# PEER expert layer: the second products of the last four expert blocks by token tile, and one copy of the final norm's weights for two gathered tiles

## The chip, the core and the metric

The program runs on one core of one Trainium2 chip. The metric is the device time of one execution in microseconds. Before the change it was measured three times: 3582.51, 3587.91 and 3587.44 us, median 3587.44.

## What is computed

One decoder layer on 1024 tokens of width 1024 and a last RMSNorm: a token mixer with three branches (stick-breaking attention, sparse attention, a gated recurrence), then a layer of 16384 experts (PEER) of which each token uses 128. The change lies in the PEER layer and in the last norm. Cut to that:

```python
def peer_ffn(x, w_q, sub_keys, u_tab, v_tab):
    ...
        eidx = jnp.take_along_axis(cand_idx, pos, axis=-1)
        gate = jax.nn.softmax(best_s, axis=-1)
        ug = u_tab[eidx]
        vg = v_tab[eidx]
        hpre = jnp.einsum("nd,nhkd->nhk", xc, ug).astype(f32)
        act = (gate * jax.nn.gelu(hpre, approximate=False)).astype(x.dtype)
        return jnp.einsum("nhk,nhkd->nd", act, vg)
...
        x = x + peer_ffn(h, peer_w_q[l], peer_sub_keys[l], peer_u[l], peer_v[l])
    return rms_norm(x, norm_final)
```

## The kernel before

The tokens lie in four parts of 256, that is eight tiles of 128. The mixer handles the parts one after the other. The PEER layer is computed in two ways at the same time.

**Tiles 2 to 5 (512 tokens) are dense.** All 16384 experts are computed for them, in 128 blocks of 128 experts (the loop of L1409). The first product of a block (`gemm1`, L1380) loads 512 KB of the table u, splits it into two f16 halves (`split`, L210: the high half on ACT, L213, the rest on DVE, L214), runs 24 matmuls of 128x512 (L258) and a Gelu on ACT (L1390). It runs three blocks ahead of the rest (LEAD). Then the block's rows of v are loaded (`vraw`, two buffers) and split the same way (`vs`, a tile with the tag "v", six buffers); DVE multiplies the Gelu's result by the gates (L1424, "the gating" below), which are mostly zero and come from DRAM in `gt` tiles for eight blocks (three buffers); the result is split into `ac` (five buffers). The second product (`gemm2`, L1427) adds the block to the output: for a token tile t of the four and a half dh of the width, three matmuls. Six of the eight outputs of 128x512 have a PSUM bank of their own (`accs`) that collects over all 128 blocks, 18 matmuls a block. The fourth tile (t = 3) has none: every four blocks, 24 matmuls go into a bank of the first products' pool (`ps_mm`), ACT copies it out (L1440) and DVE adds it to `acc7` (L1441). After the loop, for t = 0 to 3, DVE adds the scaled output to the residual `yd` (L1460), `rms_scale` (L218 to L233) forms the norm's factor with a square on ACT (L223) and steps of 128x1 on DVE and ACT, DVE multiplies by the factor and the weights `gfd` (L1462), and SP stores (L1463).

**Tiles 0, 1, 6 and 7 gather** (`gather_tile`, L1133). For each of its 128 columns an indirect DMA, issued by POOL, fetches for every token the row of u that it uses (L1145, 512 KB), and DVE multiplies it with the token's vector and sums it up (L1147). ACT applies the Gelu (L1149), DVE the gates (L1151). Then 128 rows of v come in the same way (L1155), and DVE adds each into `gacc` (L1157). The norm follows (L1160), with its weights loaded into `gf` (L1161), the multiply (L1162) and the store (L1163). Tiles 6 and 7 run beside the second half of the dense loop, one after the other. Their rows rotate through eleven buffers (`late_rows`, L1075): four of five with the tag "rows", four halves of two larger tiles (named `rr_u`, `rr_v`), and three freed tiles. The tag "rows" also holds `gh2`, `gacc`, the square's junk and `gf`.

**What sets the order.** Each engine executes one list in order. The lists are laid out when the kernel is built: the framework's scheduler simulates the program with its own costs, picks what is ready, and inserts the waits. A buffer that comes free later moves everything that wants it, and all that the scheduler places after it. Lines under `paced()` (the gathers' DVE operations) are further held to a pace.

Of the kernel before, what the change touches and what calls it, by code (L numbers as in the profile page):

```python
# [10 lines left out]
F32 = mybir.dt.float32  # L11
# [5 lines left out]
AF = mybir.ActivationFunctionType  # L17
ALU = mybir.AluOpType
# [16 lines left out]
D = 1024  # L35
TH = 512
# [28 lines left out]
PARTS = [Part(i, i * 256, 256) for i in range(4)]  # L65
# [6 lines left out]
def trunk(ctx: ExitStack, tc: tile.TileContext, a: dict, out: bass.AP):  # L72
    nc = tc.nc
    V, S, G, P = nc.vector, nc.scalar, nc.gpsimd, nc.tensor
# [10 lines left out]
    ps_mm = ctx.enter_context(tc.tile_pool(name="ps_mm", bufs=2, space=PSUM))  # L85
# [9 lines left out]
    def log_exp():  # L95

        tc.keep_in_program_order(S.preload_act_table_set(LOG_EXP))

    def load(t, src):
        nc.sync.dma_start(t, src)  # L100
        return t

    def W4(name, shape=(128, 1024), dt=F32):
        return w4.tile(list(shape), dt, tag="w4", name=name)

    def W2(name, shape=(128, 512), dt=F32, tag="at", bufs=AT):
        return (wk if tag in ("at", "pre", "sg") else w2).tile(list(shape), dt, tag=tag, name=name, bufs=bufs)
# [103 lines left out]
    def split(hi, lo, src, scale):  # L211

        S.activation(hi, src, AF.Copy, scale=scale)  # L213
        V.scalar_tensor_tensor(lo, in0=src, scalar=scale, in1=hi, op0=ALU.mult, op1=ALU.subtract)  # L214
# [855 lines left out]
    def rows(name):  # L1070
        return gat.tile([128, D], F32, tag="rows", name=name, bufs=RB)
# [43 lines left out]
    def paced():  # L1115

        if not paces:
            def rows(tau):
                return [tau * (p + PB) if k >= PACE0 else 0.0 for k, (_, v, p) in enumerate(marks)]

            lo, hi = 0.0, 10.0
            for _ in range(40):
                mid = (lo + hi) / 2
                lo, hi = (mid, hi) if sum(rows(mid)) < PACE else (lo, mid)
            acc = 0.0
            for m, r in zip(marks, rows(lo)):
                acc += r
                paces.extend([m[0]] * (int(acc) - len(paces)))
            paces.append(marks[-1][0])
            paces.append(0)  # L1130
        k = paces[-1]
        paces[-1] += 1
        return tc.issue_after(paces[min(k, len(paces) - 2)])  # L1133

    def gather_tile(ti):
        row = late_rows if ti // 2 == PARTS[-1].i else rows
        h2 = load(rows(f"gh2_{ti}"), d_h2[ti])
        idx = load(gat.tile([128, 128], I32, tag="gidx", name=f"gidx_{ti}", bufs=1), d_idx[ti])
        gate = load(gat.tile([128, 128], F32, tag="ggate", name=f"ggate_{ti}", bufs=2), d_gate[ti])
        hpre = gat.tile([128, 128], F32, tag="hpre", name=f"hpre_{ti}", bufs=1)  # L1140
        G.memset(hpre, 0.0)
        act = gat.tile([128, 128], F32, tag="act", name=f"act_{ti}", bufs=1)
        for c in range(128):
            ur = row(f"u{ti}_{c}")
            G.indirect_dma_start(out=ur, out_offset=None, in_=a["peer_u"], in_offset=bass.IndirectOffsetOnAxis(ap=idx[:, c:c + 1], axis=0))  # L1145
            with paced():
                V.scalar_tensor_tensor(ur, in0=ur, scalar=1.0, in1=h2, op0=ALU.mult, op1=ALU.mult, accum_out=hpre[:, c:c + 1])  # L1147
        with tc.high_priority():
            S.activation(act, hpre, AF.Gelu)  # L1149
            log_exp()  # L1150
        V.tensor_tensor(act, act, gate, op=ALU.mult)  # L1151
        acc = load(rows(f"gacc_{ti}"), d_x2[ti])
        for c in range(128):
            vr = row(f"v{ti}_{c}")
            G.indirect_dma_start(out=vr, out_offset=None, in_=a["peer_v"], in_offset=bass.IndirectOffsetOnAxis(ap=idx[:, c:c + 1], axis=0))  # L1155
            with paced():
                V.scalar_tensor_tensor(acc, in0=vr, scalar=act[:, c:c + 1], in1=acc, op0=ALU.mult, op1=ALU.add)  # L1157
        with tc.high_priority():
            log_exp()
        y = rms_scale(acc, f"fin{ti}", rows(f"sqf{ti}"), "g")  # L1160
        gf = load(rows(f"gf{ti}"), a["norm_final"].to_broadcast([128, D]))  # L1161
        V.scalar_tensor_tensor(acc, in0=acc, scalar=y, in1=gf, op0=ALU.mult, op1=ALU.mult)  # L1162
        nc.sync.dma_start(out[ti * 128:(ti + 1) * 128, :], acc)  # L1163

# [35 lines left out]
    NI = 128  # L1200
# [64 lines left out]
    for pt in PARTS:  # L1265
        i = pt.i
# [73 lines left out]
    t = 0  # L1340
# [41 lines left out]
    def gemm1(i):  # L1382

        ge = W2(f"ge{i}")
        ps = ps_mm.tile([128, TH], F32, tag="mm", name=f"g1_{i}")
        raw = load(W4(f"uraw{i}", (128, 8, 128)), a["peer_uT"][i])
        u = wpl.tile([128, 2, 8, 128], F16, tag="wp", name=f"us{i}", bufs=WB)
        split(u[:, 0], u[:, 1], raw, SW)
        mm3(ps, (u[:, 0], u[:, 1]), (h2[:, 0], h2[:, 1]), 8)
        S.activation(ge, ps, AF.Gelu, scale=1.0 / (SW * SH2))  # L1390
        return ge
# [8 lines left out]
    accs = [ps_a.tile([128, 512], F32, name=f"acc{i}") for i in range(6)]  # L1400
    acc7 = late.tile([128, 2, 512], F32, name="acc7")
    V.memset(acc7, 0.0)
    group = []
# [2 lines left out]
    gts = {}  # L1406
    ys = []
    gone = 0
    for k, i in enumerate(order):  # L1409
        if k + LEAD < NI:  # L1410
            ges[order[k + LEAD]] = gemm1(order[k + LEAD])
        raw = load(late.tile([128, D], F32, tag="vraw", name=f"vraw{i}", bufs=2), a["peer_v"][i * 128:(i + 1) * 128, :])
        v = late.tile([128, 2, D], F16, tag="v", name=f"vs{i}", bufs=6)
        split(v[:, 0], v[:, 1], raw, SW)
        if i // 8 not in gts:
            gts[i // 8] = []
            for c in (0, 16):
                gt = late.tile([128, 16, 8, 16], F32, tag="gt", name=f"gt{i}_{c}", bufs=3)
                nc.sync.dma_start(gt, d_G[c:c + 16, :, i // 8 * 8:i // 8 * 8 + 8, :].rearrange("c p i n -> p c i n"))
                gts[i // 8].append(gt)  # L1420
        ge = ges.pop(i)
        for c, gt in enumerate(gts[i // 8]):
            gv = ge[:, c * 256:c * 256 + 256].rearrange("p (c n) -> p c n", n=16)
            V.tensor_tensor(gv, gv, gt[:, :, i % 8, :], op=ALU.mult)  # L1424
        ac = late.tile([128, 2, TH], F16, tag="ac", name=f"ac{i}", bufs=5)
        split(ac[:, 0], ac[:, 1], ge, 1.0)
        group.append((ac, v))  # L1427

        def gemm2(ps, t, dh, ac, v, start, stop):
            for n, (x, y) in enumerate(((0, 0), (0, 1), (1, 0))):  # L1430
                P.matmul(ps, ac[:, x, t * 128:(t + 1) * 128], v[:, y, dh * 512:(dh + 1) * 512], start=start and n == 0, stop=stop and n == 2)  # L1431

        for u in range(6):
            if u in (2, 4) and len(group) == 4:
                d0 = u // 2 - 1
                ps = ps_mm.tile([128, TH], F32, tag="mm", name=f"g2_{i}_{u}")
                for n, (x, y) in enumerate(group):
                    gemm2(ps, 3, d0, x, y, n == 0, n == 3)
                part = W2(f"p7_{i}_{u}")
                S.activation(part, ps, AF.Copy)  # L1440
                V.tensor_tensor(acc7[:, d0], acc7[:, d0], part, op=ALU.add)  # L1441
                if d0:
                    group = []
            gemm2(accs[u], u // 2, u % 2, ac, v, k == 0, k == NI - 1)

        if k + LEAD >= NI:
            ys.append(load(W4(f"yd{len(ys)}"), d_x2[DENSE[0].ti0 + len(ys)]))
            if k == NI - 1:
                ys.append(load(W4("yd3"), d_x2[DENSE[0].ti0 + 3]))
                gfd = load(late.tile([128, D], F32, tag="v", name="gfd", bufs=6), a["norm_final"].to_broadcast([128, D]))  # L1450

        while ending and gone < (k + 1) * TP:
            ending.pop(0).emit(1 << 20)
            gone += 1
    log_exp()
    for t in range(4):
        y = ys[t]
        for dh in range(2):
            yv = y[:, dh * 512:(dh + 1) * 512]
            V.scalar_tensor_tensor(yv, in0=(accs[t * 2 + dh] if t < 3 else acc7[:, dh]), scalar=1.0 / (SW * SA), in1=yv, op0=ALU.mult, op1=ALU.add)  # L1460
        r = rms_scale(y, f"find{t}", late.tile([128, D], F32, tag="vraw", name=f"sqd{t}", bufs=2))
        V.scalar_tensor_tensor(y, in0=y, scalar=r, in1=gfd, op0=ALU.mult, op1=ALU.mult)  # L1462
        nc.sync.dma_start(out[TD + t * 128:TD + (t + 1) * 128, :], y)  # L1463
# [96 lines left out]
```

## Time and profile before

| | us |
|---|---|
| median of three runs | 3587.44 |
| lowest and highest | 3582.51, 3587.91 |
| the profiled execution | 3598.97 |
| its span in the profile | 3597.2 |
| PE busy | 3273.4 (91%) |
| DVE busy | 3002.8 (83%) |
| ACT busy | 1588.9 (44%) |
| POOL busy | 1342.3 (37%) |

The profile is of one execution, 11.53 us longer than the median of the others; 1.8 us of it lie outside the span. PE is the matmul engine, DVE the vector engine, ACT the one for activations, POOL issues the gathers and SP the other loads and stores. A busy share over the whole span says little here: the stages have different limits, and the stretch that the change touches is the last 300 us or so, in which PE, DVE and the DMA engines are all nearly full.

### The profile page before, as it was taken

To read this page: it belongs to the slowest core of one execution; us is meant where nothing else is said; L and a number is where in the kernel's file an instruction comes from. 1 tells how busy PE (TensorE), PEld (TensorE's weight loads), DVE (VectorE), ACT (ScalarE), POOL (GpSimd) and SP (SyncE) were. 2 spreads that over 40 slices of the span, in tenths; PEclk is the share of its full clock that TensorE was granted. 3 is DMA by queue.
4 is the path that set the end of the run, shared out by engine and by line. 5 is a ranking of instruction groups with operands and counts; after the bars stand their busy time and mean duration, and the time that the engine had idled before them with its cause. 6 is when DMAs were issued, how large, how long until landed. Compare 5 with 4: busy or idle time off the path is not lost.

```text
span 3597.2 us, 57076 instructions
## 1 busy us (share of the span) xinstructions
PE 3273.4 (91%) x20660; PEld 2191.4 (61%) x20660; DVE 3002.8 (83%) x6662; ACT 1588.9 (44%) x3157; POOL 1342.3 (37%) x1166
## 2 busy tenths in 40 slices
PE   7999989989997889999878879879999999999997
PEld 6887777778875667787666645434444444444443
DVE  5565678888799878788997777999897998898898
ACT  5776455653443554645356333224233333333333
POOL 0000002343323323223332233346674765666664
PEclk9999999999996889999677789989999999999998
DMA  8964856989977577887665799789998999999997
GB/s 300 329 237 143 303 185 224 329 300 328 351 259 230 198 248 244 306 320 261 218 201 184 265 348 316 240 270 374 358 369 316 383 378 343 379 358 364 352 343 263
DMA packets 358760, 1053.88 MB, mean 293 GB/s; under 512 B 35174, under 2 KB 107562, under 8 KB 354380
## 3 DMA queue, kind: packets, MB, share of 16 engines
q0 software_dynamic: 147456, 536.94, 41.7%
q1 hardware_dynamic: 211020, 513.29, 40.2%
q8 instruction: 162, 2.65, 0.3%
q14 instruction: 122, 1.00, 0.1%
HBM read 942.09 MB, written 108.00 MB: 292 GB/s over the span
## 4 chain that ended last, share of the span: by engine, by line
PE 44%; DVE 24%; DMA 11%; issue 10%; ACT 7%; POOL 4%; SPq 0%; POOLq 0%; DVEq 0%; ACTq 0%
PE g L258 11%; PE acc L1431 8%; DVE u L1147 4%; PE pj_mg L258 3%; DVE gacc L1157 3%; PE g L1431 3%; DMA d_G<-stage 3%; PE pj_r_hg L258 3%; DMA v<-in_peer_v_dram,gidx 2%; PE pb L258 2%; DMA u<-in_peer_u_dram,gidx 2%; PE pj_wo L258 2%; POOL v L1155 2%; DMA gt<-d_G 1%; POOL u L1145 1%
## 5 line engine op out<-in xcount | busy, mean ns | idle before, releaser
L1155 POOL DMA_INDIRECT v<-in_peer_v_dram,gidx x421 | 541.5, 1286 | 723.1 <-DVE gacc L1157 435.6
L1145 POOL DMA_INDIRECT u<-in_peer_u_dram,gidx x417 | 523.7, 1256 | 683.2 <-DVE u L1147 440.2
L258 PE MATMUL g<-h,us 128*128 128x512 f16 x3072 | 692.0, 382 | 26.3 <-DVE ts L982 10.3
L1157 DVE SCALAR_TENSOR_TENSOR gacc<-v,act,gacc 128x1024 f32<-128x1024 f32 x421 | 538.5, 1279 | 35.1 <-DMA v<-in_peer_v_dram,gidx 31.6
L1431 PE MATMUL acc<-vs,ac 128*128 128x512 f16 x2304 | 540.3, 383 | 23.1 <-DVE vs L214 9.7
L1431 PEld LDWEIGHTS <-ac 128*128 128x128 f16 x3072 | 303.2, 99 | 419.2 <-issue 58.7
L258 PEld LDWEIGHTS <-us 128*128 128x128 f16 x3072 | 302.1, 98 | 395.3 <-issue 24.8
L1147 DVE SCALAR_TENSOR_TENSOR u<-u,gh 128x1024 f32<-128x1024 f32 x417 | 501.6, 1218 | 33.1 <-DMA u<-in_peer_u_dram,gidx 30.0
L1390 ACT ACTIVATE ge<-g 128x512 f32<-128x512 f32 x128 | 76.2, 595 | 570.6 <-PE g L258 528.2
L258 PE MATMUL pj_mg<-hT,w_mg 128*128 128x256 f16 x2304 | 276.3, 276 | 8.8 <-ACT mg L883 7.0
L258 PEld LDWEIGHTS <-w_mg 128*128 128x128 f16 x2304 | 228.7, 100 | 40.1 <-issue 12.6
L1431 PE MATMUL g<-vs,ac 128*128 128x512 f16 x768 | 187.4, 386 | 24.6 <-ACT ge L1390 23.0
L1221 ACT ACTIVATE stage<-gb 128x512 f32<-128x512 f32 x128 | 130.3, 1070 | 125.3 <-DMA d_G<-stage 59.9
L214 DVE SCALAR_TENSOR_TENSOR vs<-vraw,vs 128x1024 f16<-128x1024 f32 x128 | 155.5, 1218 | 35.5 <-ACT vs L213 35.3
L213 ACT ACTIVATE vs<-vraw 128x1024 f16<-128x1024 f32 x128 | 133.0, 1046 | 82.4 <-DMA vraw<-in_peer_v_dram 79.6
L258 PE MATMUL pb<-o,w_b 128*128 128x256 f16 x1152 | 147.8, 286 | 21.4 <-DVE sg L921 12.7
L1145 POOL DMA_INDIRECT rr_u<-in_peer_u_dram,gidx x95 | 132.6, 1396 | 85.6 <-DVE rr_u L1147 62.7
L1155 POOL DMA_INDIRECT rr_v<-in_peer_v_dram,gidx x90 | 128.6, 1428 | 95.5 <-DVE gacc L1157 72.4
L214 DVE SCALAR_TENSOR_TENSOR us<-uraw,us 128x1024 f16<-128x1024 f32 x128 | 155.9, 1218 | 9.8 <-ACT us L213 9.4
L1218 PE MATMUL gb<-hot 128*128 128x128 f16 x512 | 125.3, 294 | 42.1 <-ACT stage L1221 22.3
L213 ACT ACTIVATE ac<-ge 128x512 f16<-128x512 f32 x128 | 79.7, 627 | 176.0 <-DVE ge L1424 122.3
L1424 DVE TENSOR_TENSOR ge<-ge,gt 128x256 f32<-128x256 f32 x256 | 98.6, 422 | 68.0 <-ACT ge L1390 46.2
(1143 smaller groups left out, 6439.4 us busy)
## 6 DMA issues: line engine op xcount, KB each, us to landing
uraw<-in_peer_uT_dram SPq DMA_DIRECT2D x128, 512.0 KB
vraw<-in_peer_v_dram SPq DMA_DIRECT2D x128, 512.0 KB
w_mg<-dw SPq DMA_DIRECT2D x72, 512.0 KB
d_G<-stage SPq DMA_DIRECT2D x32, 1024.0 KB
gt<-d_G SPq DMA_DIRECT2D x32, 1024.0 KB
w_r_hg<-dw SPq DMA_DIRECT2D x36, 512.0 KB
w_b<-dw SPq DMA_DIRECT2D x72, 256.0 KB
wr_mg<-in_wblk_dram SPq DMA_DIRECT2D x24, 512.0 KB
```

Source lines behind the costliest of these rows:

```text
L213: S.activation(hi, src, AF.Copy, scale=scale)
L214: V.scalar_tensor_tensor(lo, in0=src, scalar=scale, in1=hi, op0=ALU.mult, op1=ALU.subtract)
L258: P.matmul(ps, l[:, k, :], r[:, k, :], start=(i == 0), stop=(i == n - 1))
L1145: G.indirect_dma_start(out=ur, out_offset=None, in_=a["peer_u"], in_offset=bass.IndirectOffsetOnAxis(ap=idx[:, c:c + 1], axis=0))
L1147: V.scalar_tensor_tensor(ur, in0=ur, scalar=1.0, in1=h2, op0=ALU.mult, op1=ALU.mult, accum_out=hpre[:, c:c + 1])
L1155: G.indirect_dma_start(out=vr, out_offset=None, in_=a["peer_v"], in_offset=bass.IndirectOffsetOnAxis(ap=idx[:, c:c + 1], axis=0))
L1157: V.scalar_tensor_tensor(acc, in0=vr, scalar=act[:, c:c + 1], in1=acc, op0=ALU.mult, op1=ALU.add)
L1218: P.matmul(ps[:, n, :], hs[:, 0, :, n], hs[:, 2, :, n], start=True, stop=False)
L1221: S.activation(stage[0][:, :, m0:m0 + 4].rearrange("p i n -> p n i"), ps, AF.Copy, scale=SA / SGT)
L1390: S.activation(ge, ps, AF.Gelu, scale=1.0 / (SW * SH2))
L1424: V.tensor_tensor(gv, gv, gt[:, :, i % 8, :], op=ALU.mult)
L1431: P.matmul(ps, ac[:, x, t * 128:(t + 1) * 128], v[:, y, dh * 512:(dh + 1) * 512], start=start and n == 0, stop=stop and n == 2)
```

## The change

In the last four blocks (124 to 127) the second products are no longer issued block by block. Nothing is issued for them at blocks 124 and 125. At block 126 the fourth tile (t = 3) and the first (t = 0) get the products of blocks 124, 125 and 126, 36 matmuls. At block 127 those two get block 127's (12 matmuls), ACT copies and DVE adds the fourth tile's two halves, and then the second and third tile get all four blocks (48 matmuls). The norms at the end come in the order 3, 0, 1, 2. In `gather_tile` the tiles of the last part (6 and 7) no longer load the final norm's weights for themselves, but read `gfd`, the dense tiles' copy.

```diff
-        gf = load(rows(f"gf{ti}"), a["norm_final"].to_broadcast([128, D]))
+        gf = gfd if ti // 2 == PARTS[-1].i else load(rows(f"gf{ti}"), a["norm_final"].to_broadcast([128, D]))
         V.scalar_tensor_tensor(acc, in0=acc, scalar=y, in1=gf, op0=ALU.mult, op1=ALU.mult)
...
+    pend = {}
     for k, i in enumerate(order):
...
-        for u in range(6):
+        if k >= NI - 4:
+
+            last = k == NI - 1
+            for t in ((3, 0) if k == NI - 2 else (3, 0, 1, 2) if last else ()):
+                for dh in range(2):
+                    if t == 3 and dh not in pend:
+                        pend[dh] = ps_mm.tile([128, TH], F32, tag="mm", name=f"g2_{i}_{dh}")
+                    ps = pend[dh] if t == 3 else accs[t * 2 + dh]
+                    todo_ = group if t in (1, 2) else group[3:] if last else group
+                    for x, y in todo_:
+                        gemm2(ps, t, dh, x, y, t == 3 and x is group[0][0], last and x is ac)
+                    if t == 3 and last:
+                        part = W2(f"p7_{i}_{dh}")
+                        S.activation(part, ps, AF.Copy)
+                        V.tensor_tensor(acc7[:, dh], acc7[:, dh], part, op=ALU.add)
+        for u in range(6 if k < NI - 4 else 0):
...
-    for t in range(4):
+    for t in (3, 0, 1, 2):
```

In the listings of the order a number behind a name tells buffers apart, and "x2" stands for two instructions alike. Lines after L1409 are one higher with the change, those after the new block 16 higher: L1424 is L1425, L1460 is L1476, L1462 is L1478.

DVE around the gating of block 127 (`ge_32431`), before:

```order
L1157 SCALAR_TENSOR_TENSOR gacc_35419<-v_108_35725,act_35055,gacc_35419 128x1024
L1157 SCALAR_TENSOR_TENSOR gacc_35419<-v_109_35728,act_35055,gacc_35419 128x1024
L1157 SCALAR_TENSOR_TENSOR gacc_35419<-v_110_35731,act_35055,gacc_35419 128x1024
L1157 SCALAR_TENSOR_TENSOR gacc_35419<-v_111_35734,act_35055,gacc_35419 128x1024
L1424 TENSOR_TENSOR ge_32431<-ge_32431,gt_0_32192 128x256
L1424 TENSOR_TENSOR ge_32431<-ge_32431,gt_16_32194 128x256
L1157 SCALAR_TENSOR_TENSOR gacc_35419<-v_112_35737,act_35055,gacc_35419 128x1024
L214 SCALAR_TENSOR_TENSOR vs_32465<-vraw_32463,vs_32465 128x1024
L214 SCALAR_TENSOR_TENSOR ac_32558<-ge_32431,ac_32558 128x512
L1157 SCALAR_TENSOR_TENSOR gacc_35419<-v_113_35740,act_35055,gacc_35419 128x1024
L1157 SCALAR_TENSOR_TENSOR gacc_35419<-v_114_35743,act_35055,gacc_35419 128x1024
L214 SCALAR_TENSOR_TENSOR vs_32493<-vraw_32491,vs_32493 128x1024
```

and with the change (`acc_23067` is `acc7`; L1457 adds block 123's second half of the fourth tile, `vs_32487` and `vs_32537` are the halves for blocks 126 and 127):

```order
L1157 SCALAR_TENSOR_TENSOR gacc_35417<-v_91_35676,act_35053,gacc_35417 128x1024
L214 SCALAR_TENSOR_TENSOR vs_32537<-vraw_32535,vs_32537 128x1024
L1457 TENSOR_TENSOR acc_23067<-acc_23067,p_123_4_32422 128x512
L1162 SCALAR_TENSOR_TENSOR gacc_34665<-gacc_34665,gy_fin_35035,gfd 128x1024
L1157 SCALAR_TENSOR_TENSOR gacc_35417<-v_92_35679,act_35053,gacc_35417 128x1024
L1425 TENSOR_TENSOR ge_32431<-ge_32431,gt_0_32192 128x256
L1425 TENSOR_TENSOR ge_32431<-ge_32431,gt_16_32194 128x256
L1157 SCALAR_TENSOR_TENSOR gacc_35417<-rr_v_93_35682,act_35053,gacc_35417 128x1024
L214 SCALAR_TENSOR_TENSOR ac_32542<-ge_32431,ac_32542 128x512
L1157 SCALAR_TENSOR_TENSOR gacc_35417<-rr_v_93_35682,act_35053,gacc_35417 128x1024
L1157 SCALAR_TENSOR_TENSOR gacc_35417<-rr_v_95_35687,act_35053,gacc_35417 128x1024 x2
L1157 SCALAR_TENSOR_TENSOR gacc_35417<-v_97_35692,act_35053,gacc_35417 128x1024
```

Before, `v_112` follows the gating, so 16 gathers of the second pass are left (`v_112` to `v_127`); now `v_93` follows, and 35 are left. Tile 6's multiply (L1162, on `gacc_34665`) stands just ahead of the gating; before, it stood some 470 rows earlier, right behind tile 6's norm.

POOL early in tile 7's first pass, before (a row per gather):

```order
L1145 DMA u_9_35081<-in_peer_u_dram,gidx_35049 128x1024
L1145 DMA u_10_35084<-in_peer_u_dram,gidx_35049 128x1024
L1145 DMA u_11_35087<-in_peer_u_dram,gidx_35049 128x1024
L1145 DMA rr_u_12_35090<-in_peer_u_dram,gidx_35049 128x1024 x2
L1145 DMA rr_u_14_35095<-in_peer_u_dram,gidx_35049 128x1024 x2
L1145 DMA u_16_35100<-in_peer_u_dram,gidx_35049 128x1024
L1145 DMA u_17_35103<-in_peer_u_dram,gidx_35049 128x1024
L1145 DMA u_18_35106<-in_peer_u_dram,gidx_35049 128x1024
```

and with the change:

```order
L1145 DMA u_9_35079<-in_peer_u_dram,gidx_35047 128x1024
L1145 DMA u_10_35082<-in_peer_u_dram,gidx_35047 128x1024
L1145 DMA rr_u_12_35088<-in_peer_u_dram,gidx_35047 128x1024 x2
L1145 DMA rr_u_14_35093<-in_peer_u_dram,gidx_35047 128x1024 x2
L1145 DMA u_16_35098<-in_peer_u_dram,gidx_35047 128x1024
L1145 DMA u_17_35101<-in_peer_u_dram,gidx_35047 128x1024
L1145 DMA u_18_35104<-in_peer_u_dram,gidx_35047 128x1024
L1145 DMA u_11_35085<-in_peer_u_dram,gidx_35047 128x1024
L1145 DMA u_19_35107<-in_peer_u_dram,gidx_35047 128x1024
```

`u_11` and the rows after it in the shared tag have moved behind gathers with higher numbers. At the pass's end the rows so put off (`u_97` to `u_99`, `u_107` to `u_110`, `u_118` to `u_121`) stand behind `u_127`, in turns of three and more, where before the pass ended with `u_127`.

DVE's last rows, before:

```order
L230 TENSOR_TENSOR u_find_32683<-y_find_32680 128x1
L233 TENSOR_TENSOR y_find_32662<-y_find_32662,u_find_32665 128x1
L231 TENSOR_TENSOR u_find_32683<-u_find_32683,ms_find_32678 128x1
L1462 SCALAR_TENSOR_TENSOR yd_32611<-yd_32611,y_find_32662,gfd 128x1024
L232 TENSOR_SCALAR u_find_32683<-u_find_32683 128x1
L233 TENSOR_TENSOR y_find_32680<-y_find_32680,u_find_32683 128x1
L1462 SCALAR_TENSOR_TENSOR yd_32613<-yd_32613,y_find_32680,gfd 128x1024
```

and with the change:

```order
L1157 SCALAR_TENSOR_TENSOR gacc_35417<-v_123_35766,act_35053,gacc_35417 128x1024
L1157 SCALAR_TENSOR_TENSOR gacc_35417<-v_124_35769,act_35053,gacc_35417 128x1024
L1157 SCALAR_TENSOR_TENSOR gacc_35417<-v_125_35772,act_35053,gacc_35417 128x1024
L1157 SCALAR_TENSOR_TENSOR gacc_35417<-rr_v_126_35775,act_35053,gacc_35417 128x1024 x2
L225 TENSOR_SCALAR gms_fin_35785<-gss_fin_35782 128x1
L230 TENSOR_TENSOR gu_fin_35790<-gy_fin_35787 128x1
L231 TENSOR_TENSOR gu_fin_35790<-gu_fin_35790,gms_fin_35785 128x1
L232 TENSOR_SCALAR gu_fin_35790<-gu_fin_35790 128x1
L233 TENSOR_TENSOR gy_fin_35787<-gy_fin_35787,gu_fin_35790 128x1
L1162 SCALAR_TENSOR_TENSOR gacc_35417<-gacc_35417,gy_fin_35787,gfd 128x1024
```

Before, the dense tiles' final multiplies (L1462) are last, and tile 7's (L1162) stands ahead of them; now the dense tiles are done earlier, between gathers, and tile 7's last gathers, its norm and its multiply come last. On PE the last first product (block 127's) stands, now as before, right behind block 123's second products, and the 96 second products of blocks 124 to 127 come after it.

## Rows read from the trace of the kernel before

**Rows 1.** Stretches: PE, PEld, DVE, ACT, POOL busy (count), PE clock, DMA, GB/s.

```profile
3200.00:3300.00 100.00, 100.00 (x465) 45.30 (x463) 91.19 (x147) 31.04 (x41) 69.41 (x45) 1.00 1.00 367
3306.00:3328.00 22.00, 20.06 (x94) 9.00 (x92) 15.77 (x19) 6.64 (x10) 8.98 (x8) 1.00 0.95 367
3328.50:3548.70 220.20, 211.56 (x957) 94.67 (x956) 201.60 (x210) 65.06 (x88) 138.10 (x104) 0.98 0.95 346
3548.70:3593.40 44.70, 23.98 (x96) 9.94 (x95) 40.69 (x64) 16.67 (x30) 9.84 (x10) 0.79 0.54 210
```

**Rows 2.** Waits of PE from 3300 us on: total us, times, longest.

```profile
PE acc L1431 <- DVE vs L214: 9.7, 3, 6.7
PE acc L1431 <- ACT vs L213: 7.7, 3, 4.1
```

**Rows 3.** Waits of DVE from 3300 us on, same columns.

```profile
DVE vs L214 <- ACT vs L213: 10.0, 2, 8.7
...
DVE ge L1424 <- DMA gt<-d_G: 6.8, 1, 6.8
```

**Rows 4.** Waits of POOL from 3000 us on, same columns.

```profile
POOL rr_u L1145 <- DVE rr_u L1147: 42.3, 12, 15.5
```

**Rows 5.** Chain of waits, four transfers: start, us, what.

```profile
3035.88 27.22 DMA gt<-d_G
...
2380.24 6.03 DMA v<-in_peer_v_dram,gidx
...
3478.25 11.50 DMA v<-in_peer_v_dram,gidx
...
3299.00 5.16 DMA vraw<-in_peer_v_dram
```

**Rows 6.** Timeline, ACT and DVE at block 127's gating: start, us, engine, line, operation.

```profile
3547.88 0.60 ACT L1390 ACTIVATE ge<-g 128x512 f32<-128x512 f32 x1 [5.45 <-PE g L258]
...
3548.74 0.75 DVE L1424 TENSOR_TENSOR ge<-ge,gt 128x256 f32<-128x256 f32 x2
```

**Rows 7.** Timeline, DVE behind it, same columns.

```profile
3549.41 1.28 DVE L1157 SCALAR_TENSOR_TENSOR gacc<-v,act,gacc 128x1024 f32<-128x1024 f32 x1
...
3550.60 1.22 DVE L214 SCALAR_TENSOR_TENSOR vs<-vraw,vs 128x1024 f16<-128x1024 f32 x1
...
3561.31 6.57 DVE L1157 SCALAR_TENSOR_TENSOR gacc<-v,act,gacc 128x1024 f32<-128x1024 f32 x5
...
3586.41 0.23 DVE L230 TENSOR_TENSOR u_find<-y_find 128x1 f32<-128x1 f32 x2
```

**Rows 8.** Groups of DVE's instructions after 3548.7 us: busy, mean ns, idle before.

```profile
L1460 DVE SCALAR_TENSOR_TENSOR yd<-acc,yd 128x512 f32<-128x512 f32 x8 | 5.3, 685 | 1.1 <-PE acc L1431 1.1
...
L1462 DVE SCALAR_TENSOR_TENSOR yd<-yd,y_find,gfd 128x1024 f32<-128x1024 f32 x4 | 5.0, 1280 | 0.0
...
L1441 DVE TENSOR_TENSOR acc<-acc,p 128x512 f32<-128x512 f32 x2 | 1.4, 684 | 0.0
```

**Rows 9.** Timeline, tile 7's norm and the end.

```profile
3575.22 1.06 ACT L223 ACTIVATE sqf<-gacc 128x1024 f32<-128x1024 f32 x1 [9.38 <-DVE gacc L1157]
...
3576.40 0.15 DVE L225 TENSOR_SCALAR gms_fin<-gss_fin 128x1 f32<-128x1 f32 x1 [1.22 <-ACT sqf L223]
...
3584.55 1.28 DVE L1162 SCALAR_TENSOR_TENSOR gacc<-gacc,gy_fin,gf 128x1024 f32<-128x1024 f32 x1
...
3592.09 1.28 DVE L1462 SCALAR_TENSOR_TENSOR yd<-yd,y_find,gfd 128x1024 f32<-128x1024 f32 x1
```

**Rows 10.** Timeline, twelve second products at two places.

```profile
3557.05 2.75 PE L1431 MATMUL acc<-vs,ac 128*128 128x512 f16 x12
...
3569.07 5.28 PE L1431 MATMUL acc<-vs,ac 128*128 128x512 f16 x12 [6.67 <-DVE vs L214]
```

**Rows 11.** Timeline, SP's two late loads of the norm's weights.

```profile
3556.48 0.45 SPq L100 DMA_DIRECT2D gfd<-in_norm_final_dram  x1
...
3567.90 0.33 SPq L100 DMA_DIRECT2D gf<-in_norm_final_dram  x1
```

## The prediction

> **What bounds the kernel now.** I read the stretches first, then the waits of each engine, then the timeline of the last 50 us. Until 3300 us TensorE is the bound: it is busy for 100.00 of 100 us with 465 matmuls, 0.215 each, while VectorE (DVE) has 91.19 us of work [rows 1]. After that DVE catches up: in the 220.2 us from 3328.5 to 3548.7 PE holds 957 matmuls, which at 0.215 would need 205.8, and DVE is busy for 201.6. The rest of PE's time is waits for the two halves of `vs`, and clock lost behind them [rows 1, 2]. DVE itself waits for loads, through ACT's half of `vs` and for `gt` [rows 3], and in that list there is no wait on a gather; POOL waits for DVE instead, since a gather needs a row buffer that DVE has to read empty [rows 4]. So DVE executes an order fixed at build time, PE is at most 16 us from full, and where a row of DVE stands in that order decides when it runs.
>
> The last 48.5 us are DVE's too. Its gating multiply of the last block (127) is at 3548.74, 0.26 us after ACT's Gelu [rows 6], and the span ends at 3597.2. DVE is busy for 40.69 of 44.70 us there, PE for 23.98 [rows 1].
>
> **Part one, the second products by token tile.** It adds and removes no matmul: 96 before, 96 now (36 at block 126, 12 + 48 at block 127), and no copy or add. In DVE's order all `vs` halves now stand ahead of block 127's gating; before, two of four came after it, waiting for loads. PE begins the 96 right behind the last first product: 96 x 0.215 = 20.6 us, so it ends about 19.4 us after the gating. DVE's last read of an accumulator is, added up from its rows, about 20.8 us after the gating. So PE is hidden by some 1.4 us, and the 6.67 us in which PE now waits for a late `vs` [rows 10] goes. By itself that would be a gain, had DVE nothing else to do.
>
> **Part two, the shared weights.** It removes two loads of 0.5 MB. Tile 7's own was issued at 3567.90 [rows 11] and used at 3584.55 [rows 9], so it is hidden and worth 0; tile 6's lay in a stretch with PE full, also 0. But `gfd` is loaded at the very end (issued at 3556.48 [rows 11]), into a slot of block 122's `vs`, and tile 6's last multiply reads it. That multiply moves from tile 6's end to just ahead of block 127's gating. Until then `gacc_6` keeps one of the five buffers with the tag "rows", and tile 7 gathers with 10 buffers where it had 11. Each turn that needs the missing one is put off: the POOL order shows `u_11` behind `u_18`. The eleven put-off rows come after `u_127`, three buffers at a time. Counting DVE's rows, tile 7's two passes are 19 gathers behind when block 127 is gated: 35 of the second pass are left, before 16.
>
> **Term B, after block 127's gating.** 35 gathers at 1.315 (five take 6.57) are 46.0; 18 of them are followed by another operation, and such a one frees DVE after 1.19 (3549.41 to 3550.60) [rows 7]: less 18 x 0.12 = 2.2, so 43.8. The gating 0.75 [rows 6]; one half of `ac`, about 0.65; the two adds to `acc7` 1.4, eight `yd` 5.3, four final multiplies 5.0 [rows 8]; twenty 128x1 operations at some 0.08 (the second of a pair of 0.23 [rows 7]), 1.6. Together 58.5, of which overlaps of neighbours give back about 0.8 (the eight `yd` take 0.63 each where they follow each other): 57.7. Then tile 7's norm, which is now the last chain: square and its sum 1.06 + 0.16 until DVE's mean (3575.22 to 3576.40 [rows 9]), then two ACT steps and five short ones on DVE, 1.4 by their rows: 2.6. Its multiply 1.28, and a store: the last multiply of before ends at 3593.37 [rows 9] and the span at 3597.2, 3.83. Sum 57.7 + 2.6 + 1.3 + 3.8 = 65.4, where 48.5 stood: **+17.0**. There is no cover for this, as DVE has no gap in it, and what stood behind PE before (the four dense tiles' norms) is now between the gathers.
>
> **Term A, before it.** The same 19 gathers are missing ahead of the gating. From DVE's 201.6 go 19 x 1.3 = 24.7, and three `vs` halves (3.4) and tile 6's multiply (1.3) come in: 181.6 if all fell into this stretch. Nine of the 19 are behind already where it begins, which leaves about 193.7. Either way PE, at 205.8, is then the longer one. The most that can be won is all of PE's lost time from 3306 on: 22.0 - 94 x 0.215 = 1.8, and 220.2 - 205.8 = 14.4 [rows 1]: **16.2**. The least is nothing, if the loads set the stalls: DMA is at 0.95 of its time there [rows 1], and part of the waits is for ACT's half of `vs`, that is for `vraw` [rows 2, 3]. I take half, **-8**: the deferred gathers relieve DVE and the DMA queues alike, but the profiled run (3598.97) is 11.5 us above the median of the runs, so the others may have less of this to win.
>
> Three new waits stand inside A, each priced at 0 with bounds. (1) `gfd` ahead of block 127's gating: its slot comes free late in block 123's second products; a load of that size took 5.16 [rows 5], and the last first product (24 x 0.215 = 5.2) and the Gelu (0.60 [rows 6]) run in that time: 0 to 3. Behind it on DVE stand the gating, and so `ac` and PE's last 60 matmuls. (2) The tail of the first pass, three buffers a turn: DVE has 7.6 to 10.4 us of other work between giving a buffer back and needing it filled, and a gather took 6.03 to 11.50 in the chain [rows 5]: 0 to 5 short, in two turns, 0 to 10. PE's three blocks of lead (3 x 42 matmuls x 0.215 = 27 us) cover it, so 0. (3) `gt`: between the last use of the old slot and the first need of the new one, DVE's order has 11.1, 7.6 and 8.9 us of work at blocks 104, 112 and 120, before 18.5, 14.8 and 20.1; one such load took 27.22 [rows 5], of which DVE felt 6.8 in the other stretch [rows 3]. 0 to 10, and 0 taken, for the same lead.
> For (2) the Trainium skill has a price: "DMA: Bandwidth & Descriptors", in the section on the anatomy of one DMA of the gpsimd path, fits 2.0 us plus the bytes over 436e3. By that a row gather of 512 KB takes an estimated 3.2 us, wait (2) is nothing, and the sum stays as it is; the trace's 6.03 to 11.50 disagree, with the queues as full as here.
>
> **The sum.** +17.0 - 8 = +9.0 against the profiled 3598.97; put on the median, 3587.44 + 9.0 = **3596.4 us**. A measurement here tells 0.2%, 7.2 us, from no change.
>
> **Rivals.**
> First, **not slower**: with DVE relieved PE's stalls all vanish, in the last 24 blocks; A is 16.2, net +0.8, about 3588. For it: the stalls are on `vs`, half of which is DVE's [rows 2]. Against: DMA at 0.95. It decides from A = 9.8 on (17.0 - 7.2), that is if block 127's gating comes before 3539 in the profile. Chance 0.30.
> Second, **the new waits are felt**: DVE stands still for `u`, `gt` or `gfd` with 27 us of lead used up, 5 to 15 us, while A gives 0 to 5: +17 to +30, about 3608. For it: a load of 27.22 and gathers of 11.50 [rows 5]. Against: DVE has never waited for a gather here. Chance 0.18.
> Third, **PE falls to the low clock** ahead of the 96: the last `vs` halves come late or the gating does, PE idles some us, and the products of tiles 1 and 2 run at 0.44 us instead of 0.215, as the twelve in 5.28 us did after 6.67 us of idling, where the same twelve took 2.75 before [rows 10]. 60 x 0.225 = 13.5 us more, of which 1.4 are hidden: some +12 on top of +9, about 3608. Against: PE's order leaves no gap, with no second product waiting at blocks 124 and 125. Chance 0.07.
> The Trainium skill ("TensorE: Matmul & The Clock Gate", Part 1 on the clock gate) says the low clock is the default, which activity releases; the two rows of twelve agree with it.
> Fourth, that it gets **faster** by more than 7.2: PE cannot give back more than 16.2 against 17.0, so B would have to be too large by 8, say with fewer gathers left at the gating than the order has, which a fixed order excludes: 3580 or less. Chance 0.07, for what one profile does not show.
>
> **How the numbers follow.** The forecast itself, net +4 to +14, has 0.38; below +7.2 lies 0.07 of it. Slower: 0.31 + 0.18 + 0.07 = 0.56. Same: 0.30 + 0.07 = 0.37. Faster: 0.07. The range goes from 3585 (the first rival less the runs' own spread of some 3 us) to 3610 (A at 0 with 5 us of new waits, +22); out of it are most of the fourth rival and the second's upper half. Of the forecast's own case the range is 3591 to 3601.
>
> **What would show it.** In the profile of the changed kernel: 35 gathers of the second pass on DVE behind block 127's gating, tile 7's multiply as DVE's last operation, and PE done 15 us or more before DVE. Gating to end should be 65 us; if it is under 60, term B is wrong. The gating's own time says what A was: 3540 in the forecast, 3532 in the first rival, after 3549 in the second, where DVE's waits must name a gather, `gt` or `gfd`. Twelve matmuls in 5.28 us behind the gating would show the third. A gating after 3549 without such waits, or a gather among DVE's waits in the last 40 us, makes the reasons wrong even if the time is right.

## The result, and the profile of the changed kernel

The changed kernel takes 3617.61 us (median of six, 3613.35 to 3623.96) where the kernel before takes 3584.98 (six, 3575.88 to 3592.22): a ratio of 1.0094, interval [1.0076, 1.0112]. It is slower by some 33 us. The forecast was 3596.4, in a range of 3585 to 3610, so the sign was right and the size was not: the time lies outside the range.

The busy time of each engine by stretch answers to [rows 1]. The second stretch runs from the gating of block 104 to that of block 127, the third from there to the last operation:

```profile
core 0: us, PE busy (x) PEld busy (x) DVE busy (x) ACT busy (x) POOL busy (x), PEclk, DMA share, GB/s
3200.00:3280.00 80.00, 80.00 (x372) 36.24 (x371) 69.17 (x112) 26.76 (x36) 53.37 (x36) 1.00 0.95 347
3283.60:3549.80 266.20, 251.33 (x1141) 112.31 (x1140) 214.52 (x236) 78.39 (x105) 140.03 (x100) 0.97 0.89 308
3549.80:3611.70 61.90, 13.99 (x64) 5.81 (x61) 59.24 (x79) 10.67 (x24) 31.84 (x28) 0.66 0.73 268
```

The first profile of before was long by chance (3598.97 against a median of 3584.98), so the same two stretches are shown from a second one, of an execution with a span of 3583.7:

```profile
3280.50:3535.20 254.70, 245.06 (x1125) 110.29 (x1124) 231.90 (x249) 78.71 (x105) 159.88 (x118) 0.99 0.96 353
3535.20:3580.00 44.80, 23.79 (x96) 9.89 (x95) 40.71 (x64) 16.71 (x30) 9.87 (x10) 0.82 0.54 211
```

Two places lose. Behind block 127's gating the last stretch has grown from 44.8 to 61.9, which with the store makes 48.5 and 65.7: that is term B, +17.2. And ahead of it the 23 blocks take 266.2 instead of 254.7, +11.5, though DVE is busy for 17.4 us less (214.52 for 231.90). DVE stands idle for 51.7 of these us, where it was 22.8. Together that is 28.7 of the 32 us between the two spans. What DVE waits for from 3300 us on, beside [rows 3] (total, times, longest):

```profile
DVE gacc L1157 <- DMA v<-in_peer_v_dram,gidx: 27.4, 9, 6.6
DVE ge L1425 <- DMA gt<-d_G: 12.6, 2, 8.2
DVE vs L214 <- ACT vs L213: 2.1, 4, 1.3
```

Before, DVE waited on no gather from 3300 us on; now nine such waits make 27.4 us. The timeline of DVE between 3300 and 3550 us shows where (start, duration, operation, and in brackets the idle time before it):

```profile
3330.58 1.28 DVE L1157 SCALAR_TENSOR_TENSOR gacc<-v,act,gacc 128x1024 f32<-128x1024 f32 x1 [1.60 <-DMA v<-in_peer_v_dram,gidx]
...
3354.18 1.28 DVE L1157 SCALAR_TENSOR_TENSOR gacc<-v,act,gacc 128x1024 f32<-128x1024 f32 x1 [2.33 <-DMA v<-in_peer_v_dram,gidx]
...
3388.20 1.28 DVE L1157 SCALAR_TENSOR_TENSOR gacc<-v,act,gacc 128x1024 f32<-128x1024 f32 x1 [1.27 <-DMA v<-in_peer_v_dram,gidx]
...
3418.73 1.28 DVE L1157 SCALAR_TENSOR_TENSOR gacc<-v,act,gacc 128x1024 f32<-128x1024 f32 x1 [6.00 <-DMA v<-in_peer_v_dram,gidx]
...
3443.22 1.28 DVE L1157 SCALAR_TENSOR_TENSOR gacc<-v,act,gacc 128x1024 f32<-128x1024 f32 x1 [4.39 <-DMA v<-in_peer_v_dram,gidx]
```

Counted along DVE's list these are `v_4`, `v_15`, `v_26`, `v_37`, `v_48`, and the other four are `v_59` to `v_92`: every eleventh. Tile 7's rows are dealt out in turns of eleven, four of which take the shared tag "rows". With `gacc_6` held, that tag has three buffers left for four rows. So the fourth, `v_48` say, takes the buffer of `v_45` of the same turn and must wait until that has been read, and on POOL it is put behind `v_55`:

```
L1155 DMA rr_v_49_35558<-in_peer_v_dram,gidx_35047 128x1024 x2
L1155 DMA rr_v_51_35563<-in_peer_v_dram,gidx_35047 128x1024 x2
L1155 DMA v_53_35568<-in_peer_v_dram,gidx_35047 128x1024
L1155 DMA v_54_35571<-in_peer_v_dram,gidx_35047 128x1024
L1155 DMA v_55_35574<-in_peer_v_dram,gidx_35047 128x1024
L1155 DMA v_48_35555<-in_peer_v_dram,gidx_35047 128x1024
L1155 DMA v_56_35577<-in_peer_v_dram,gidx_35047 128x1024
```

DVE adds the rows into `gacc` in order, so it needs `v_48` right after `v_47`. The timeline of that turn (`v_44` to `v_47` are read from 3431.75, `v_48` at 3443.22; POOL's row is the issue of `v_48`):

```profile
3431.75 5.28 DVE L1157 SCALAR_TENSOR_TENSOR gacc<-v,act,gacc 128x1024 f32<-128x1024 f32 x4
3436.95 0.75 DVE L1425 TENSOR_TENSOR ge<-ge,gt 128x256 f32<-128x256 f32 x2
3437.62 1.22 DVE L214 SCALAR_TENSOR_TENSOR us<-uraw,us 128x1024 f16<-128x1024 f32 x1
```

```profile
3435.55 0.98 POOL L1155 DMA_INDIRECT v<-in_peer_v_dram,gidx  x1 [0.30 <-issue]
```

`v_45` is read by 3434.4 (two of the four in 5.28 us), `v_48` is issued at 3435.55 and used at 3443.22, 7.7 us later, and DVE has work until 3438.8 only. The DMA engines are no fuller than before: their share fell from 0.96 to 0.89. Nor do gathers take longer: from issue to landing the median of those into `v` in this stretch is 7.2 us, where the second run below, which has no such wait, has 8.5. What is missing is time between the read of `v_45` and the need of `v_48`.

### The profile page after: what moved, and what is told of

Its sections match the earlier page's. It is cut to its first block, busy times and chain, and to the rows that moved or that the text cites. A ratio compares the mean times of both kernels' runs of the same rounds, so it can differ in the third digit from the quotient of the medians.

```text
span 3615.5 us, 57067 instructions
## 1 busy us (share of the span) xinstructions
PE 3271.9 (90%) x20660; PEld 2189.8 (61%) x20660; DVE 3001.6 (83%) x6662; ACT 1586.1 (44%) x3155; POOL 1351.7 (37%) x1166
## 4 chain that ended last, share of the span: by engine, by line
PE 43%; DVE 24%; issue 12%; DMA 10%; ACT 7%; POOL 4%; SPq 0%; POOLq 0%; DVEq 0%; ACTq 0%
PE g L258 10%; PE acc L1432 7%; DVE gacc L1157 4%; PE pj_mg L258 4%; DMA v<-in_peer_v_dram,gidx 3%; DVE u L1147 3%; PE g L1432 2%; PE pj_r_hg L258 2%; PE pb L258 2%; DMA d_G<-stage 2%; POOL u L1145 2%; PE pj_wo L258 2%; DMA u<-in_peer_u_dram,gidx 2%; POOL v L1155 1%; ACT stage L1221 1%
## 5 line engine op out<-in xcount | busy, mean ns | idle before, releaser
L1432 PE MATMUL acc<-vs,ac 128*128 128x512 f16 x2304 | 530.6, 381 | 2.5 <-ACT ac L213 2.5
L258 PEld LDWEIGHTS <-w_mg 128*128 128x128 f16 x2304 | 229.4, 101 | 40.7 <-issue 12.8
L258 PE MATMUL pb<-o,w_b 128*128 128x256 f16 x1152 | 146.7, 284 | 22.8 <-DVE sg L921 14.7
L1425 DVE TENSOR_TENSOR ge<-ge,gt 128x256 f32<-128x256 f32 x256 | 97.8, 419 | 79.3 <-ACT ge L1390 50.4
```

The source lines that it names most:

```text
L258: P.matmul(ps, l[:, k, :], r[:, k, :], start=(i == 0), stop=(i == n - 1))
```

## The experiments

**The two parts apart.** H is the theory of the hold: `gacc_6` waits for `gfd` and takes a buffer from tile 7. Its rivals are P, that the products by token tile make the loss, and S, that the sharing of the weights as such does.

The weights alone:

```diff
-        gf = load(rows(f"gf{ti}"), a["norm_final"].to_broadcast([128, D]))
+        gf = gfd if ti // 2 == PARTS[-1].i else load(rows(f"gf{ti}"), a["norm_final"].to_broadcast([128, D]))
```

> Only the shared weights; the second products stay block by block. Theory H (hold): gacc_6 waits for gfd until block 127's gating, tile 7 has three shared row buffers for four rows a turn, so in its second pass one gather in eleven is issued out of turn and DVE waits for it. H expects the whole loss here: 3610 to 3620 us against some 3585 of before, 35 gathers behind block 127's gating, 20 to 30 us of DVE waits on v gathers after 3300 us. Rival P (the products by tile make the loss): within 7 us of before.

Measured: 3622.19 us, ratio 1.0106 [1.0085, 1.0126]. The whole loss is here, 2 us above the range expected, with 35 gathers behind block 127's gating, and in this run the list of DVE's waits from 3300 us on begins with

```profile
DVE gacc L1157 <- DMA v<-in_peer_v_dram,gidx: 26.6, 9, 6.5
DVE ge L1424 <- DMA gt<-d_G: 11.9, 2, 8.5
```

The products alone, against the changed kernel:

```diff
-        gf = gfd if ti // 2 == PARTS[-1].i else load(rows(f"gf{ti}"), a["norm_final"].to_broadcast([128, D]))
+        gf = load(rows(f"gf{ti}"), a["norm_final"].to_broadcast([128, D]))
```

> Only the second products by token tile; tiles 6 and 7 load their own weights. H: no wait on a gather in the second pass, 16 gathers behind block 127's gating, DVE's work behind it about 36.6 us and 5 more to the end, 41.5 where before has 48.5: 7 us less than before, 3575 to 3583. Rival P: 3605 or more, with PE waiting at blocks 126 and 127.

Measured: 3587.31 us, ratio 1.0011 [0.9992, 1.0030]: no loss, no gather waits, 16 gathers behind the gating. P falls. But the gain that was expected is not there either. From the gating to the end its profile has 52.9 us, not 41.5, which is 4.4 more than the 48.5 of before, and PE ends 32 us behind the gating, as before. Its waits of PE from 3300 us on name the reason, the same as in [rows 2]:

```profile
PE g L1432 <- DVE vs L214: 7.2, 2, 6.7
```

The change, with `gfd` for tile 7 alone, against the changed kernel:

```diff
-        gf = gfd if ti // 2 == PARTS[-1].i else load(rows(f"gf{ti}"), a["norm_final"].to_broadcast([128, D]))
+        gf = gfd if ti == 7 else load(rows(f"gf{ti}"), a["norm_final"].to_broadcast([128, D]))
```

> The change, but only tile 7 reads gfd; tile 6 loads its own copy, as before. H: as the products alone, within 5 us, no gather waits: 3575 to 3584. Rival S (the sharing itself, a late gfd or its slot, makes the loss): more than 3605.

Measured: 3587.41 us, ratio 1.0001 [0.9986, 1.0015], no gather waits; the time is above the range expected, as in the run before it. S falls: a tile that reads `gfd` at the program's end, where it is there anyway, loses nothing. The loss is tile 6's alone, whose multiply has to wait for `gfd`. The load of tile 7 that is removed here has no price that can be told (3587.31 us with it, 3587.41 without).

**Too few buffers, or one out of turn?** The whole change, with `gacc_6` still held, but tile 7's rows are dealt out over ten buffers, three of them with the shared tag:

```diff
-        j = taken[0] % (RB + 6)
+        short = taken[0] >= 256
+        j = (taken[0] - 256) % (RB + 5) if short else taken[0] % (RB + 6)
         taken[0] += 1
...
-        j -= RB - 1
+        j -= RB - 2 if short else RB - 1
```

> The whole change, gacc_6 still held, but tile 7's rows rotate over ten buffers (three with the shared tag) and so come in turn. H (the out-of-turn row is what costs): gather waits of DVE under 5 us after 3300, 22 gathers behind block 127's gating, so 50 us from there to the end: 3583 to 3597. Rival N (ten buffers instead of eleven are too few, in turn or not): still 20 us and more of gather waits, 3605 to 3620.

Measured: 3580.34 us, ratio 0.9984 [0.9967, 1.0001]. The gather waits are gone, though tile 7 has the same ten buffers and `gacc_6` is held even longer: its multiply now stands behind the gating of block 127, at 3541.99. What has changed is that every row takes a buffer that was read ten gathers before, where the row out of turn took one that was read three before. N falls. Its two stretches, from block 104's gating on and from block 127's, are

```profile
3278.60:3519.50 240.90, 240.90 (x1118) 109.18 (x1116) 222.79 (x239) 78.12 (x105) 150.22 (x112) 1.00 0.98 360
3519.50:3566.00 46.50, 18.78 (x87) 8.33 (x85) 44.97 (x68) 11.06 (x25) 14.88 (x15) 0.73 0.68 244
```

PE has no gap up to the gating: the stretch is 13.8 us shorter than in the second profile of before, and to the end of the span it is 50.4 us, as its count of 22 gathers gave. This is term A as it was meant: 1118 matmuls at 0.215 make 240.4, so of PE's lost time 0.5 us is left. The medians show less of it than this one profile, 4.5 us, and the interval holds no change; the time is below the range expected, and the profiled execution (3571.67) was itself 8.7 us below the median of its run.

**What the products by token tile are worth.** First the same ten buffers with the second products block by block (the kernel before with the first and the last of the diffs above, the one on `gf` and the one on the rotation):

> Both tiles read gfd and tile 7's rows rotate over ten buffers in turn, as in the fourth run, but the second products stay block by block. H: no gather waits again, 22 gathers behind block 127's gating, 50 us from there to the end, 3575 to 3590. Theory Z (DVE's work behind the gating sets the end, so the order of PE's last 96 products is worth nothing): within 5 us of the fourth run's 3580.3. Rival Q (the products by tile are worth something once their inputs are early): 5 us or more above it.

Measured: 3579.50 us, ratio 0.9985 [0.9968, 1.0002], within 1 us of the run above, again without gather waits and with 22 gathers and 49.5 us behind the gating. Z stands, Q falls: with DVE setting the end, the order of PE's last 96 matmuls is worth nothing that can be told.

Then the late `vs` halves, with the last two `vraw` in a buffer of `gt` that is free from block 119 on:

```diff
-        raw = load(late.tile([128, D], F32, tag="vraw", name=f"vraw{i}", bufs=2), a["peer_v"][i * 128:(i + 1) * 128, :])
+        if k == NI - 2:
+            vpair = late.tile([128, 2, D], F32, tag="gt", name="vpair", bufs=3)
+        if k >= NI - 2:
+            raw = vpair[:, k - NI + 2]
+            nc.sync.dma_start(raw, a["peer_v"][i * 128:(i + 1) * 128, :])
+        else:
+            raw = load(late.tile([128, D], F32, tag="vraw", name=f"vraw{i}", bufs=2), a["peer_v"][i * 128:(i + 1) * 128, :])
```

in the third run, in the kernel before, and in the fourth:

> The third run (products by tile, only tile 7 shares) with the rows of v of blocks 126 and 127 loaded into a gt buffer that has been free since block 119, so that their halves no longer wait for the two vraw buffers. Theory D (the products by tile gained nothing because their last two inputs come late): PE ends 20 to 25 us behind block 127's gating instead of 31, from the gating to the end 44 to 47 us instead of 52.9, 3577 to 3583. Rival: the loads themselves are late (DMA), PE still ends 30 us behind the gating and the time stays at 3587.

> The kernel before with the same spare buffer for the rows of v of blocks 126 and 127; products block by block, own weights. D: PE ends 22 to 26 us behind block 127's gating instead of 32, 44 to 47 us from the gating to the end instead of 48.5, 3579 to 3585, and within 3 us of the run with the products by tile. Q: the run with the products by tile is 4 us or more below this one.

> The fourth run (whole change, ten buffers in turn) with the spare buffer too. Its vs halves were early already, and 25 gathers instead of 22 stand behind block 127's gating: by DVE's work 4 us longer behind the gating, 53 to 55 us, and PE not waited for; 3580 to 3590. Rival: with the loads out of the way block 127's gating comes earlier by more than that, 3570 to 3578.

Measured: 3587.30 us, ratio 1.0009 [0.9993, 1.0025], with the products by tile; 3586.27, 1.0004 [0.9987, 1.0020], block by block; 3582.23, 1.0004 [0.9986, 1.0022], on ten buffers. The mechanism of D is there: PE ends 22.7 us behind the gating in the first two (31.3 and 31.9 without the spare buffer), and from the gating to the end it is 45.2 and 45.0 us, 53.4 in the third, each as counted beforehand. The time does not follow: the first two lie above the ranges expected, and none of the three can be told from before, whose median is 3583.05 beside them. In the profile of the first of the three PE's waits from 3300 us on show 10.8 us lost to other `vs` halves,

```profile
PE acc L1438 <- ACT vs L213: 10.8, 3, 4.7
```

where its parent, the third run, had 6.4: in that profile part of what is won behind the gating is missing elsewhere. Why the medians of the first two show no gain stays open. Whether the two earlier loads push the other ones back was not tried. Block by block and by tile are 1 us apart again.

**Second profiles.**

> The kernel before, unchanged, for a second profile. If the first profile was long by chance (3597 where the runs have 3585), the spread lies ahead of the end: block 0's gating at 2122 to 2137 us instead of 2143, 245 to 255 us from block 104's gating to block 127's instead of 258.6, and again 48 to 49 from there to the end. If the first profile shows the rule, 2143 and 258 come back.

> The changed kernel, unchanged, for a second profile. H: again some nine DVE waits on a v gather, 20 to 30 us together, 262 to 270 us from block 104's gating to block 127's, block 127's first product done 15 us or more ahead of its gating, and 65 to 67 us from there to the end. A rival (the gather waits of the first profile were chance): under 10 us of such waits.

Measured: the kernel before 3585.5 us, with 254.8 us from block 104's gating to block 127's and 48.5 behind it; ahead of that, block 0's gating is at 2141.5, so that part of the expectation failed: what made the first profile long lay later, between the gatings of block 0 and block 127. The changed kernel 3613.58, with 265.7 and 65.6, and in the list of DVE's waits from 3300 us on

```profile
DVE gacc L1157 <- DMA v<-in_peer_v_dram,gidx: 26.4, 9, 6.4
```

The gather waits are the rule. Behind block 127's gating the two profiles of each kernel agree within 0.1 us; what varies lies ahead of it. From block 104's gating to block 127's the six profiles with tile 7's rows in the old order (before twice, the second, third, sixth and seventh run) take 246.2 to 260.8 us. The three with one row in eleven out of turn take 264.5 to 266.3, and the three with ten buffers in turn 240.9 to 243.2. So the loss and term A both stand out of this spread, but one pair of profiles does not size either of them closely.

## Why the prediction was wrong

**Term B was right.** 35 gathers stood behind block 127's gating, tile 7's multiply was DVE's last operation, and 65.7 us (65.6 in the second profile) went from the gating to the end, where the sum had 65.4. The end of the timeline answers to [rows 9]:

```profile
3605.05 2.60 DVE L1157 SCALAR_TENSOR_TENSOR gacc<-rr_v,act,gacc 128x1024 f32<-128x1024 f32 x2
3607.69 1.06 ACT L223 ACTIVATE sqf<-gacc 128x1024 f32<-128x1024 f32 x1 [29.53 <-DVE gacc L1157]
...
3610.30 1.28 DVE L1162 SCALAR_TENSOR_TENSOR gacc<-gacc,gy_fin,gfd 128x1024 f32<-128x1024 f32 x1
```

**Term A had the wrong sign**, -8 where it was +11.5 (block 104 to 127, against the second profile of before; +7.6 against the first, on which the sum was made). The step that failed is "Either way PE, at 205.8, is then the longer one", together with wait (2), which priced the three buffers in the first pass only. DVE's work in the stretch did shrink as forecast, by 17.4 us where the prediction had 8 to 20. But the gathers' work that left it did not leave DVE free: DVE waited there, 27.4 us, for nine of the gathers that stayed. In the first pass a late row can be overtaken, since each column has its own sum, and the scheduler let others go first: the one wait on a `u` was 0.7 us. In the second pass all rows go into one `gacc` in order. There the same shortage came back as a wait of 1.3 to 6.6 us per turn, nine times. The listing of POOL's order showed `v_15`, `v_26` and so on behind rows seven numbers higher; it was read for the first pass and not for the second. The sentence that the list of waits of before has no gather in it was true, and said nothing of a kernel in which a buffer is read only three gathers before it is needed again.

PE's first products, meanwhile, came as early as the forecast wanted. Block 127's first product is done by 3528.0, 6.4 us earlier than in the second profile of before (3534.4) though that execution's end came 32 us earlier. But the gating followed 21.8 us behind it instead of 0.9, because DVE had not reached it. PE did not go straight on with the 96 second products either. It stood for 9.43 us for a copy by ACT (L1456), which came behind a row of ACT that waited 13.56 us for DVE's gating of block 126. The timeline of PE, and then that of DVE, in the changed kernel:

```profile
3522.65 5.34 PE L258 MATMUL g<-h,us 128*128 128x512 f16 x24
3537.43 2.29 PE L1432 MATMUL g<-vs,ac 128*128 128x512 f16 x5 [9.43 <-ACT p L1456]
```

```profile
3526.64 1.28 DVE L1157 SCALAR_TENSOR_TENSOR gacc<-v,act,gacc 128x1024 f32<-128x1024 f32 x1 [6.58 <-DMA v<-in_peer_v_dram,gidx]
...
3548.63 1.28 DVE L1157 SCALAR_TENSOR_TENSOR gacc<-v,act,gacc 128x1024 f32<-128x1024 f32 x1 [1.41 <-DMA v<-in_peer_v_dram,gidx]
3549.83 0.81 DVE L1425 TENSOR_TENSOR ge<-ge,gt 128x256 f32<-128x256 f32 x2
```

**The three new waits.** `gfd`: DVE did not wait for it, but it came to that multiply late; in the fourth run, without gather waits, there is no such wait either, with the multiply behind the gating. The first pass's tail: 0.7 us; 0 was right. `gt`: 12.6 us from 3300 on, where before had 6.8 and 5.9 in its two profiles, so some 6 of the 0 to 10, where 0 was taken.

**The rivals.** The second, that new waits are felt, comes nearest, with 28.7 of its +17 to +30 between the profiles (32.6 between the medians), and block 127's gating at 3549.83 is where it was to be; it had 0.18. But it priced 5 to 15 us of waits on `u`, `gt` or `gfd`, and what was waited for was `v`, for 27.4 us. The reason against it, that DVE had never waited for a gather, holds only while tiles 6 and 7 gather: earlier in the first profile of before, ahead of 2390 us, DVE waits 31.6 us on rows of v and 30.0 on rows of u. What the first rival has for A came true in the fourth run, where the wait was taken away: PE full up to the gating. The third did not come: PE slowed down behind its waits, but it is done 46 us ahead of DVE's last operation (3565.2 to 3611.6). Nor did the fourth.

**Part one** was said to save the 6.67 us of PE's wait. Alone it does not (second run): that wait stays, because what ends it is DVE's row for `vs`, and this stands 19.05 us behind the gating, with nine gathers just ahead of it. Before, the `vs` rows of blocks 124 to 127 all came behind the gating, and not two of four as the prediction has it. Part two is what moved them: all four stand ahead of the gating in the first run (the weights alone), none in the second. With the spare buffer of the sixth and seventh runs two stand ahead, and PE's waits on DVE's half shrink to 0.8 us.

**The base.** The forecast set a sum made on one profile onto the median. That profile was 14 us above the median of before, and the stalls that A could win were partly its own: from block 104's gating to block 127's, 1125 matmuls (241.9 us at 0.215) leave 16.7 us in the first profile (258.6) and 12.8 in the second (254.7).

**Slips that change nothing.** In the prediction 65.4 less 48.5 is 16.9, not 17.0; 181.6 and nine gathers at 1.3 make 193.3, not 193.7. Of the two gathers that the prediction holds against a price of 3.2 us, the one of 6.03 lay at 2380 us, in a stretch with a DMA share of 0.79, not as full as at the end; the one of 11.50 did lie there.

## What to carry to other kernels

A tile that is kept alive longer costs what its buffer was doing. Here a load of 0.5 MB that nobody waited for was saved, and its user had to hold one of five buffers for some 530 us (its multiply is at 3545.95, where before has it at 3019.11). When a rotation loses a buffer, look at every consumer in order, and count how much work lies between a buffer's last read and its next use, against the transfer's time. Here it was some 4.4 us (3434.4 to 3438.8 in the turn shown) against a median of 7.2. Ten buffers in turn cost no wait on a gather, ten buffers with one row in eleven out of turn 27 us of them. And a term of the form "this engine has less work now" is not a gain until its list has been read for new waits.

## What was not expected of the hardware

A gather that was issued 7.7 us ahead of its use still came late (3435.55 to 3443.22), with the DMA share at 0.89 in that stretch. That is no outlier: the median there is 7.2 us, and 8.5 in the second run with a share of 0.98. And executions of one kernel differ by more than any edit here but the sharing of tile 6's weights in the old rotation: 35 of the kernel before, taken beside the fifth to eighth runs, lie between 3563.51 and 3602.47 us. In its two profiles the whole difference lies ahead of block 127's gating, and the stretch behind it took 48.5 us in both.
